# The low half of split weight chunks: negated high half plus an accumulating DMA in place of a VectorE subtraction

## The chip, the cores and the metric

The kernel runs on one core of one Trainium2 chip. The metric is the device time of one execution in microseconds (us); the engines' work is read from a hardware profile of one execution. Engines are named as in the profile: PE is TensorE (PEld its weight loads), DVE VectorE, ACT ScalarE, POOL GpSimd, SP SyncE.

## The reference, cut to what matters

One decoder block on 16 meta tokens and 512 tokens of width 1024. Every large step is a float32 matrix product with a weight matrix:

```python
hn = rmsnorm(h, norm1_g); p = hn @ w_in          # q, k, v, glr, r, u, ga, gb
o = rmsnorm(gla_chunked(q, k, v, log_a)); y_a = (o * silu(r)) @ w_a
y_b = (multiscale_pool(u) @ w_pool_grp * pool_scale) @ w_b
h = h + (sigmoid(ga) * y_a + sigmoid(gb) * y_b) @ w_o
up = causal_dwconv(rmsnorm(h, norm2_g) @ w_up); a, b = split(up)
h = h + (silu(a) * b) @ w_down
out = rmsnorm(h, final_norm_g)
```

## The kernel before, in words

Activations lie transposed, features on the 128 partitions and 528 positions along the row. The weights are cut on the host into 142 chunks `wts[j]` of 128 x 1024 float32 (512 KB): 8 blocks of 128 x 128 that make one block of 128 output features. The order of the chunks, `ORDER`, is k 0-3, q 4-7, v 8-15, r 16-23, u 24-31, ga 32-39, a 40-47, gb 48-55, grp 56-57, b 58-65, o 66-73, up 74-117, down 118-141. In the down stage three chunks make one output block, and the third of the three has only 6 blocks (`nk = 6`, 384 KB).

PE multiplies rounded numbers (`F32R`), so each operand is split into a rounded high part and the rest: `hi = round(w)`, `lo = w - hi`. `products` issues for each block hi x activation-hi, hi x activation-lo and lo x activation-hi, twice each for the two halves of the positions: 48 matmuls for a chunk, the low half needed first by the fifth of them.

The preparation of chunk j is a chain. SP loads `wts[j]` into a raw tile (`wraw`, three buffers); ACT copies it, rounded, into `whi`; DVE subtracts into `wlo` (`whi` and `wlo` have three buffers each). `chunk(j)` prepares chunks up to j + 2 (`PREP_AHEAD`) and loads up to j + 5. So the buffers of chunk j + 2 come free when PE is through with chunk j - 1, that is, as it begins chunk j, and the chain has two chunks' worth of PE time to end. Instructions on one engine run in the order the scheduler of the tile framework gave them, and each waits for its operands by semaphores.

POOL has little to do before the change: constants at the start, the running sums of the pooling branch (line 500, tiles `pt`, 10 additions from the tiles `u` over some 46 us in the u and ga stages), and sums of squares for the last two norms (lines 574 and 627).

Of the kernel before, what the change touches and what calls it, by code (L numbers as in the profile page):

```python
# [13 lines left out]
ALU = mybir.AluOpType  # L14
# [7 lines left out]
KT = 8  # L22
# [23 lines left out]
ORDER = {}  # L46
# [10 lines left out]
def f32(ap):  # L57
    return ap.bitcast(F32)
# [3 lines left out]
def hybrid_block(ctx: ExitStack, tc: tile.TileContext, xt, g1d, wts, wglr, wgk, vecs, out):  # L62
    nc = tc.nc
    act, dve, pool, pe, sp = nc.scalar, nc.vector, nc.gpsimd, nc.tensor, nc.sync
# [19 lines left out]
    def load_chunk(j, cuts=None):  # L84
        if j >= NCHUNK or (j in raws and cuts is None):
            return
        nk = 6 if j >= ORDER["down"] and (j - ORDER["down"]) % 3 == 2 else KT
        if j not in raws:
            raws[j] = (wrawp.tile([P, KT, P], F32, tag="wraw", name=f"wraw{j}"), nk)
        for a, b in cuts or ((0, nk),):  # L90
            sp.dma_start(raws[j][0][:, a:b], wts[j, :, a:b])

    def prep_chunk(j, cuts=None):
        if j >= NCHUNK or (j in preps and cuts is None):
            return
        load_chunk(j)
        t, nk = raws[j]
        if cuts is None or cuts[0] == 0:
            preps[j] = tuple(whlp.tile([P, KT, P], F32R, tag=f"w{n}", name=f"w{n}{j}") for n in ("hi", "lo"))
        hi, lo = preps[j]  # L100
        a, b = cuts or (0, nk)
        act.activation(hi[:, a:b], t[:, a:b], AF.Copy)  # L102
        dve.tensor_tensor(lo[:, a:b], t[:, a:b], f32(hi[:, a:b]), ALU.subtract)  # L103

    def chunk(j, ahead=PREP_AHEAD):
        for i in range(j, j + ahead + 1):
            prep_chunk(i)
        for i in range(j, j + RAW_AHEAD + PREP_AHEAD + 1):
            load_chunk(i)
        return preps[j]  # L110
# [71 lines left out]
    for k in range(KT):  # L182
        for a, b in FULL if k == 0 else ((0, L),):
            act.activation(xh[:, k, a:b], x0[:, k, a:b], AF.Copy, scale=g1[:, k : k + 1])
            dve.scalar_tensor_tensor(xl[:, k, a:b], x0[:, k, a:b], g1[:, k : k + 1], f32(xh[:, k, a:b]), ALU.mult, ALU.subtract)
        for cut in {0: ((0, 2),), 1: ((2, 5),), 3: ((5, 8),)}.get(k, ()):
            prep_chunk(0, cut)
            prep_chunk(1, cut)
        if k >= 2:
            act.activation(sq1[:, k - 2], x0[:, k - 2], AF.Square)  # L190
# [76 lines left out]
    for k in range(KT):  # L267
        for m in range(2):
            hi, lo = preps[m]
# [215 lines left out]
    for g in range(4):  # L485
# [7 lines left out]
        for i in range(g + 1):  # L493
            d = 1 << i
            nxt = pts[g % 2][:, 2 * (2 * (g // 2) + i % 2) :][:, 0:2]
            a = starts[i]
            if a < d:
                pool.tensor_copy(nxt[:, :, a:d], cur[:, :, a:d])
                a = d
# [32 lines left out]
    for m in range(8):  # L532
        hi, lo = chunk(ORDER["grp"] + m // 4)
# [16 lines left out]
    for m in range(8):  # L550
        acc = project(f"pb{m}", ORDER["b"] + m, pbh, pbl, TAIL)
        t = gb[:, m, T0:]
# [9 lines left out]
    for m in range(8):  # L562
        acc = project(f"po2{m}", ORDER["o"] + m, mh, ml, TAIL)
        t = h2[:, m, T0:]
# [66 lines left out]
    for a, b in ((0, 256), (256, 512)):  # L631
# [8 lines left out]
        t = h3[:, 7, a:b]  # L640
# [81 lines left out]
```

## Time and profile before

| | |
|---|---|
| time, median of 3 runs | 862.53 us (862.34 to 862.57) |
| span of the profiled execution | 860.6 us, so 1.9 us of the median lie outside the span |
| PE busy | 847.6 us (98%) |
| PEld busy | 824.5 us (96%) |
| DVE busy | 485.0 us (56%), of it 175.9 us for the 146 subtractions of line 103 |
| ACT busy | 345.1 us (40%), of it 149.2 us for the 146 rounding copies of line 102 |
| POOL busy | 62.3 us (7%) |
| SP's queue of DMAs | 30.4% of the 16 DMA engines' time, 78.84 MB |

The device time of the profiled execution itself isn't given beside its span; its span stands for it, and the 1.9 us are added to it. In a row of a timeline the columns are start, duration, engine, line, operation and tiles. In a row of groups they are count, total time, mean of one, and idle time ahead of it. The row `DMA` of the page gives the busy share of the DMA engines in 40 slices, in tenths.

### The profile page before, as it was taken

How to read it: one execution, taken by the hardware profiler on the slowest of the kernel's cores; microseconds unless marked ns; L12 is line 12 of the kernel's file. 1: busy time of each engine (PE TensorE's matmuls, PEld its weight loads, DVE VectorE, ACT ScalarE, POOL GpSimd, SP SyncE). 2: the span in 40 equal slices, each digit the busy share in tenths (PEclk: the TensorE clock that was granted, in tenths of full speed). 3: DMA queues.
4: the chain of work that ended last, by engine and by line, in shares of the span. 5: the costliest groups of instructions: out<-in, count | busy, mean ns of one | idle time of the engine just before them, and what ended most of it. 6: DMA issues, size and time to landing. Idle time of an engine off the chain costs nothing.

```text
span 860.6 us, 15278 instructions
## 1 busy us (share of the span) xinstructions
PE 847.6 (98%) x6627; PEld 824.5 (96%) x6627; DVE 485.0 (56%) x716; ACT 345.1 (40%) x479; POOL 62.3 (7%) x48
## 2 busy tenths in 40 slices
PE   8999999999999999999999999999999999999995
PEld 7999999999999999999999999999999999888884
DVE  6676445389647433355554677667776777332224
ACT  6378243256335212353234544444444444232231
POOL 4000000001740000000012100000000000001011
PEclk9999999999999999999999999999999999999998
DMA  7423311122332333225332333233323332332312
GB/s 241 123 74 99 87 61 50 50 75 74 99 98 75 98 98 99 84 89 196 98 88 85 99 98 85 89 98 99 90 83 98 98 95 79 95 101 85 97 39 98
DMA packets 25939, 81.13 MB, mean 94 GB/s; under 512 B 2864, under 2 KB 5680, under 8 KB 25872
## 3 DMA queue, kind: packets, MB, share of 16 engines
q1 hardware_dynamic: 24384, 78.84, 30.4%
q10 hardware_dynamic: 1488, 1.32, 0.5%
q8 instruction: 52, 0.85, 0.4%
q14 instruction: 15, 0.12, 0.0%
HBM read 78.05 MB, written 2.10 MB: 93 GB/s over the span
## 4 chain that ended last, share of the span: by engine, by line
PE 96%; DVE 1%; ACT 1%; DMA 1%; issue 0%; SPq 0%; DVEq 0%
PE pup L119 29%; PE pv L119 5%; PE pu L119 5%; PE pr L119 5%; PE pga L119 5%; PE po L119 5%; PE pb L119 5%; PE pgb L119 5%; PE pa L119 5%; PE pd L615 5%; PE pd L614 5%; PE pd L616 5%; PE pq L119 3%; PE pk L119 1%; PE pgrp L119 1%; PE po L415 1%
## 5 line engine op out<-in xcount | busy, mean ns | idle before, releaser
L102 ACT ACTIVATE whi<-wraw 128x1024 fp32r<-128x1024 f32 (+2 forms) x146 | 149.2, 1024 | 330.2 <-PE pd L615 71.0
L103 DVE TENSOR_TENSOR wlo<-wraw,whi 128x1024 fp32r<-128x1024 f32 (+2 forms) x146 | 175.9, 1206 | 78.8 <-ACT whi L102 68.8
L119 PE MATMUL pup<-h2l,whi 128*128 128x258 f32 x704 | 141.6, 282 | 0.0
L119 PE MATMUL pup<-h2h,whi 128*128 128x258 f32 x704 | 140.9, 282 | 0.0
L119 PE MATMUL pup<-h2h,wlo 128*128 128x258 f32 x704 | 140.8, 281 | 0.0
L119 PEld LDWEIGHTS pup<-h2h,wlo 128*128 128x128 f32 x704 | 108.8, 188 | 0.0
L119 PEld LDWEIGHTS pup<-h2h,whi 128*128 128x128 f32 x704 | 107.9, 188 | 0.0
L119 PEld LDWEIGHTS pup<-h2l,whi 128*128 128x128 f32 x704 | 107.8, 188 | 0.0
L614 PE MATMUL pd<-gh,whi 128*128 128x512 f32 (+1 forms) x198 | 72.7, 367 | 0.0
L615 PE MATMUL pd<-gl,whi 128*128 128x512 f32 (+1 forms) x198 | 72.4, 365 | 0.0
L616 PE MATMUL pd<-gh,wlo 128*128 128x512 f32 (+1 forms) x198 | 72.3, 365 | 0.0
L591 DVE TENSOR_TENSOR up<-pup,rstd 128x258 f32<-128x258 f32 x88 | 33.5, 421 | 45.9 <-PE pup L119 44.5
L614 PEld LDWEIGHTS pd<-gh,whi 128*128 128x128 f32 x198 | 37.3, 189 | 6.1
L616 PEld LDWEIGHTS pd<-gh,wlo 128*128 128x128 f32 x198 | 37.3, 189 | 6.0
L615 PEld LDWEIGHTS pd<-gl,whi 128*128 128x128 f32 x198 | 37.3, 189 | 6.0
L594 ACT ACTIVATE cv<-up,vec 128x512 f32<-128x512 f32 x44 | 35.9, 816 | 3.8 <-DVE up L591 3.2
L218 ACT ACTIVATE gh<-cv 128x512 fp32r<-128x512 f32 x22 | 13.9, 633 | 55.1 <-DVE cv L600 55.1
L596 DVE SCALAR_TENSOR_TENSOR cv<-up,vec,cv 128x512 f32<-128x512 f32 x44 | 33.1, 752 | 1.5
L595 DVE SCALAR_TENSOR_TENSOR cv<-up,vec,cv 128x512 f32<-128x512 f32 x44 | 32.9, 747 | 1.3 <-ACT cv L594 1.3
L627 POOL TENSOR_TENSOR sq<-sq,n_sq 128x512 f32<-128x512 f32 x6 | 7.8, 1296 | 348.0 <-ACT n_sq L626 348.0
L598 ACT ACTIVATE cv<-cv 128x512 f32<-128x512 f32 x22 | 13.9, 633 | 41.1 <-DVE cv L596 41.1
L574 POOL TENSOR_TENSOR n_sq<-n_sq,n_sq 128x514 f32<-128x514 f32 x7 | 12.4, 1778 | 220.5 <-ACT n_sq L570 220.5
(241 smaller groups left out, 1804.5 us busy)
## 6 DMA issues: line engine op xcount, KB each, us to landing
wraw<-in_wts_dram SPq DMA_DIRECT2D x132, 512.0 KB, 3.6
wraw<-in_wts_dram SPq DMA_DIRECT2D x10, 384.0 KB, 3.1
h<-in_xt_dram SPq DMA_DIRECT2D x1, 2056.0 KB, 8.8
x<-in_xt_dram SPq DMA_DIRECT2D x7, 264.0 KB, 5.9
out_dram<-h ACTq DMA_DIRECT2D x2, 384.0 KB, 2.8
out_dram<-h ACTq DMA_DIRECT2D x2, 256.0 KB, 2.3
out_dram<-h SPq DMA_DIRECT2D x2, 256.0 KB, 2.5
x<-in_xt_dram SPq DMA_DIRECT2D x2, 132.0 KB, 2.4
```

The costliest lines, as they stand in the source:

```text
L102: act.activation(hi[:, a:b], t[:, a:b], AF.Copy)
L103: dve.tensor_tensor(lo[:, a:b], t[:, a:b], f32(hi[:, a:b]), ALU.subtract)
L119: pe.matmul(acc[:, s, : b - a], w, x[:, a:b], start=(i == 0 and w is wh and x is xh), stop=(i == n - 1 and last),)
L218: act.activation(hi, src, AF.Copy)
L591: dve.tensor_tensor(z[:, c], src, rstd2[:, c], ALU.mult)
L594: act.activation(cv, z[:, META:], AF.Identity, scale=v1("cw2", m), bias=v1("cb", m))
L595: dve.scalar_tensor_tensor(cv, z[:, META - 1 : L - 1], v1("cw1", m), cv, ALU.mult, ALU.add)
L596: dve.scalar_tensor_tensor(cv, z[:, META - 2 : L - 2], v1("cw0", m), cv, ALU.mult, ALU.add)
L598: last = act.activation(cv, cv, AF.Silu)
L614: pe.matmul(acc, hi[:, k], gh[part][:, k, a:b], start=first, stop=False)
L615: pe.matmul(acc, hi[:, k], gl[part][:, k, a:b], start=False, stop=False)
L616: pe.matmul(acc, lo[:, k], gh[part][:, k, a:b], start=False, stop=last)
```

## The change

For chunks 4 to 141, other than the eight with `nk = 6`, DVE no longer subtracts: 130 chunks. In its place the low tile is first set to minus the high tile, by DVE for even j and by POOL for odd j; then POOL issues a DMA that reads the raw chunk from HBM a second time and adds it to what stands in `wlo`. Chunks 0 to 3 and the eight shorter ones keep the subtraction. The raw load by SP and the rounding copy by ACT stay for all chunks.

```diff
         act.activation(hi[:, a:b], t[:, a:b], AF.Copy)
-        dve.tensor_tensor(lo[:, a:b], t[:, a:b], f32(hi[:, a:b]), ALU.subtract)
+        if j < ORDER["q"] or nk < KT:
+            dve.tensor_tensor(lo[:, a:b], t[:, a:b], f32(hi[:, a:b]), ALU.subtract)
+            return
+        if j % 2:
+            pool.tensor_scalar(lo, hi, -1.0, 1.0, ALU.mult, ALU.mult)
+        else:
+            dve.tensor_scalar(lo, f32(hi), -1.0, None, ALU.mult)
+        pool.dma_start(lo, wts[j], accum_op=ALU.add)
```

The new code is seven lines longer, so line 103 of before is line 104 after, and line 500 is 507. PE's and SP's instructions stand in the same order after as before. POOL's don't: it gets 65 negations (line 107) and 130 DMA issues (line 110) among its other work. The number behind a tile's name counts the program's tiles.

First POOL in the u and ga stages. Before, only the additions of the pooling branch stand there:

```order
L500 TENSOR_TENSOR pt_2581<-u 128x2x516
L500 TENSOR_TENSOR pt_2581<-pt_2581 128x2x514
L500 TENSOR_TENSOR pt_2580<-u 128x2x520
L500 TENSOR_TENSOR pt_2580<-pt_2580 128x2x518
L500 TENSOR_TENSOR pt_2580<-pt_2580 128x2x514
L498 COPY pt_2581<-u 128x2
L500 TENSOR_TENSOR pt_2581<-u 128x2x527
L500 TENSOR_TENSOR pt_2581<-pt_2581 128x2x526
L500 TENSOR_TENSOR pt_2581<-pt_2581 128x2x522
L500 TENSOR_TENSOR pt_2581<-pt_2581 128x2x514
L507 TENSOR_SCALAR pt_2581<-pt_2581 128x2
```

After, the weight chunks stand among them; wlo_2367 belongs to chunk 30 and wlo_2431 to chunk 31:

```order
L507 TENSOR_TENSOR pt_2611<-u 128x2x516
L110 DMA wlo_2367<-in_wts_dram 128x1024
L507 TENSOR_TENSOR pt_2611<-pt_2611 128x2x514
L107 TENSOR_SCALAR wlo_2431<-whi_2430 128x1024
L110 DMA wlo_2431<-in_wts_dram 128x1024
```

and a little later wlo_2627 to chunk 34 and wlo_2685 to chunk 35:

```order
L505 COPY pt_2611<-u 128x2
L507 TENSOR_TENSOR pt_2611<-u 128x2x527
L110 DMA wlo_2627<-in_wts_dram 128x1024
L507 TENSOR_TENSOR pt_2611<-pt_2611 128x2x526
L507 TENSOR_TENSOR pt_2611<-pt_2611 128x2x522
L507 TENSOR_TENSOR pt_2611<-pt_2611 128x2x514
L514 TENSOR_SCALAR pt_2611<-pt_2611 128x2
L107 TENSOR_SCALAR wlo_2685<-whi_2684 128x1024
L110 DMA wlo_2685<-in_wts_dram 128x1024
```

So the DMA of chunk 30 stands behind one long addition, and the negation and DMA of chunk 35 behind three.

At the end of the program POOL has, after the change, the negation of chunk 139 (wlo_8643) and the DMAs of chunks 139 and 140 (wlo_8648) ahead of its last sums:

```order
L107 TENSOR_SCALAR wlo_8643<-whi_8642 128x1024
L110 DMA wlo_8643<-in_wts_dram 128x1024
L110 DMA wlo_8648<-in_wts_dram 128x1024
L634 TENSOR_TENSOR sq_8084<-sq_8084,n_sq_8719 128x512
L657 TENSOR_TENSOR h_8083<-h_8083,rstd_0_8798 128x2x256
```

On DVE in the up stage a pair of chunks has two subtractions before (wlo_6494 and wlo_6559), each behind the eviction of an accumulator (`up<-pup`):

```order
L591 TENSOR_TENSOR up_0_6485<-pup_0_6436,rstd_5130 128x258
L591 TENSOR_TENSOR up_0_6485<-pup_0_6436,rstd_5130 128x256
L103 TENSOR_TENSOR wlo_6494<-wraw_6306,whi_6493 128x1024
L595 SCALAR_TENSOR_TENSOR cv_0_6488<-up_0_6485,vec,cv_0_6488 128x512
L596 SCALAR_TENSOR_TENSOR cv_0_6488<-up_0_6485,vec,cv_0_6488 128x512
L591 TENSOR_TENSOR up_1_6548<-pup_1_6499,rstd_5130 128x258
L591 TENSOR_TENSOR up_1_6548<-pup_1_6499,rstd_5130 128x256
L103 TENSOR_TENSOR wlo_6559<-wraw_6369,whi_6558 128x1024
```

After, such a pair has one negation on DVE:

```order
L598 TENSOR_TENSOR up_0_7488<-pup_0_7439,rstd_5202 128x258
L598 TENSOR_TENSOR up_0_7488<-pup_0_7439,rstd_5202 128x256
L602 SCALAR_TENSOR_TENSOR cv_0_7491<-up_0_7488,vec,cv_0_7491 128x512
L603 SCALAR_TENSOR_TENSOR cv_0_7491<-up_0_7488,vec,cv_0_7491 128x512
L598 TENSOR_TENSOR up_1_7552<-pup_1_7503,rstd_5202 128x258
L598 TENSOR_TENSOR up_1_7552<-pup_1_7503,rstd_5202 128x256
L109 TENSOR_SCALAR wlo_7563<-whi_7562 128x1024
```

The other chunk of the pair left DVE's order and stands in POOL's.

## The prediction

> **What bounds the kernel now.** The page first. Its head gives each engine's busy time, and its slices where:
>
> ```profile
> span 860.6 us, 15278 instructions
> PE 847.6 (98%) x6627; PEld 824.5 (96%) x6627; DVE 485.0 (56%) x716; ACT 345.1 (40%) x479; POOL 62.3 (7%) x48
> PE   8999999999999999999999999999999999999995
> DMA  7423311122332333225332333233323332332312
> ```
>
> PE is the bound: idle for 860.6 - 847.6 = 13.0 us, nearly all in the first and last slices. DVE, which the change relieves, is busy for half the time. The windows say how full PE is in the long stages, and the waits of PE, in the row that concerns this change, what the subtractions cost it:
>
> ```profile
> 60.00:120.00 60.00, 60.00 (x499) 60.00 (x498) 32.95 (x61) 30.18 (x71) 0.00 (x0) 1.00 0.30 88
> ...
> 522.00:600.00 78.00, 78.00 (x657) 78.00 (x656) 57.16 (x84) 34.32 (x41) 0.00 (x0) 1.00 0.31 90
> ```
>
> ```profile
> PE pk L119 <- DVE wlo L103: 0.4, 1, 0.4
> ```
>
> Columns: window, length, then busy time and count of PE, PEld, DVE, ACT, POOL, granted clock (1.00 is full), DMA share, GB/s. PE has no gap in either. It waited for a low half once, 0.4 us, on a k chunk, which the change leaves alone. PE's instructions and their order don't change. So there is next to nothing to win; the question is whether the new chain is hidden.
>
> How much time the chain has is read from the timeline of one plain chunk, in the a stage (rows of ACT, DVE and PEld):
>
> ```profile
> 281.23 1.06 ACT L102 ACTIVATE whi<-wraw 128x1024 fp32r<-128x1024 f32 x1 [1.91 <-PE pga L119]
> 281.57 0.31 PEld L119 LDWEIGHTS pa<-zh,wlo 128*128 128x128 f32 x2
> 282.32 1.23 DVE L103 TENSOR_TENSOR wlo<-wraw,whi 128x1024 fp32r<-128x1024 f32 x1 [0.15 <-ACT whi L102]
> 286.95 1.06 ACT L102 ACTIVATE whi<-wraw 128x1024 fp32r<-128x1024 f32 x1 [4.02 <-PE pa L119]
> ...
> 293.01 0.31 PEld L119 LDWEIGHTS pa<-zh,wlo 128*128 128x128 f32 x2
> ```
>
> ACT starts on a chunk as PE lets go of the old one: 281.23, and the next at 286.95, so a chunk takes 5.72 us of PE. The low half whose preparation starts here is the one first loaded at 293.01, two chunks after 281.57. DVE is done at 283.55: 9.46 us to spare.
>
> **The change, part by part.**
>
> *The subtraction goes*, the negation comes. Prices, from groups of DVE and of POOL:
>
> ```profile
> L103 DVE TENSOR_TENSOR wlo<-wraw,whi 128x1024 fp32r<-128x1024 f32 x132 | 165.3, 1253 | 73.6 <-ACT whi L102 63.6
> L646 DVE TENSOR_SCALAR h<-h,vec 128x256 f32<-128x256 f32 x2 | 0.7, 352 | 1.0 <-ACT sq L642 1.0
> L319 DVE TENSOR_SCALAR mid_p<-bn 128x16 f32<-128x16 f32 x1 | 0.2, 172 | 0.0
> L258 POOL MEMSET early_r<- 128x1024 int32 x1 | 1.0, 957 | 0.0
> L500 POOL TENSOR_TENSOR pt<-pt 128x1028 f32<-128x1028 f32 x3 | 8.8, 2931 | 0.2
> L500 POOL TENSOR_TENSOR pt<-pt 128x1036 f32<-128x1036 f32 x1 | 1.9, 1916 | 0.1
> ```
>
> DVE loses 130 x 1.25 = 163 us. A one-input TENSOR_SCALAR goes from 172 ns at 16 columns to 352 at 256, 0.75 ns a column, so 0.9 us at 1024 (bounds 0.35 and 1.25); 65 of them are 60 us. DVE ends near 380 us busy, and this buys nothing, since DVE is waited for by no one that matters. POOL's negation reads one tile: between the memset of that size (1.0) and a two-input addition of that size, 1.9 where it ran free and 2.9 where it ran beside DVE's work. I take 1.2, near the memset as it too has one stream fewer, and keep 2.9. That is 78 us of POOL, 190 at worst, spread over the span.
>
> *The raw tile* is released by ACT instead of DVE, so SP's loads start about 1.2 us sooner. SP waited long there, but the loads were far ahead, and its gain is nothing:
>
> ```profile
> SPq L91 <- DVE wlo L103: 729.5, 134, 12.5
> ```
>
> *The accumulating DMA* has no row before. The nearest are plain loads (size, count, median us from issue to landing):
>
> ```profile
> wraw<-in_wts_dram SPq DMA_DIRECT2D x132, 512.0 KB, 3.6
> ...
> h<-in_xt_dram SPq DMA_DIRECT2D x1, 2056.0 KB, 8.8
> ```
>
> From these, (8.8 - 3.6) / 1544 KB gives 1.7 us of moving for 512 KB and 1.9 us fixed. The window 522:600 agrees: 0.31 of 5.72 us is 1.77 us of all DMA engines for a load. An add reads its target as well as its source. Bounds: 3.6 us if the second read hides, 8.8 if an add costs as much as moving four times the bytes. I take twice the bytes moved, 1.9 + 3.4 = 5.3 us to land, issuing by POOL included, for that is what must be read at least; it is nearer the lower row. The DMA engines are then busy for 1.77 + 3.54 = 5.3 of each 5.72 us, 93%: full, but not over.
>
> The Trainium skill, "Collectives: The Full Stack", section "The bandwidth ceiling: the fold count and why AG ≠ RS ≠ AR", says that an add inside the DMA path costs its second source read and no more; it measured 62.28 GB/s for the copying and 32.35 for the adding collective, a ratio of 1.93. No run here shows it yet; by it the landing would be an estimated 1.9 + 1.93 x 1.7 = 5.2 us, and the sum 0.3 us less. Against the change speaks "DMA: Bandwidth & Descriptors", section "Specifications": the first byte of a DMA issued from GpSimd comes at about 1 us, from SP at about 0.6. By that the landing would be an estimated 5.7, and the sum 1.2 us more.
>
> Even chunk, on the clock of the timeline above: rounding ends at 282.29, negation 283.2, landing 288.5, needed 293.01: 4.5 us over. Odd chunk: negation by 283.5 (285.2 at worst), landing 288.8 (290.5): 2.5 us over at worst; SP's load of 1.7 us at the same time still fits. POOL has time for it: in two chunks, 11.4 us, it has one negation and two issues to do, and each issue waits only for a negation that is done by then.
>
> *Behind POOL's additions* the cover is thinner. The timeline of POOL, of DVE's eviction that the first addition waits for, and PEld's needs:
>
> ```profile
> 213.18 0.75 DVE L233 TENSOR_TENSOR u<-pu,rstd 128x260 f32<-128x260 f32 x2
> 214.08 6.38 POOL L500 TENSOR_TENSOR pt<-u 128x1032 f32<-128x1032 f32 x1 [10.06 <-DVE u L233]
> 220.54 2.76 POOL L500 TENSOR_TENSOR pt<-pt 128x1028 f32<-128x1028 f32 x1
> ...
> 236.48 1.95 POOL L500 TENSOR_TENSOR pt<-u 128x1054 f32<-128x1054 f32 x1 [0.17 <-DVE u L233]
> 238.51 8.15 POOL L500 TENSOR_TENSOR pt<-pt 128x1052 f32<-128x1052 f32 x3
> ```
>
> ```profile
> 224.07 0.31 PEld L119 LDWEIGHTS pu<-xh,wlo 128*128 128x128 f32 x2
> ...
> 252.97 0.31 PEld L119 LDWEIGHTS pga<-xh,wlo 128*128 128x128 f32 x2
> ```
>
> Chunk 30's DMA stands behind the addition that ran from 214.08 to 220.46. One subtraction less on DVE ahead of the eviction brings that end to 219.2; landing 224.5, needed 224.07: late by 0.5 us (0 if the addition takes 1.9 us, 1.7 if it isn't earlier). Chunk 31: the next addition ends at 222.0, negation 223.2, landing 228.5, needed two chunks after chunk 29's need, near 229.9: in time. Chunk 35 has three additions ahead, to 246.7, the small scaling, the negation to 248.1, landing 253.4, needed 252.97: late by 0.4 (0 to 2.1). A late chunk moves the later needs back with it, so I add only these two.
>
> *At the end* the chunks are shorter for PE and nothing follows that could make up. ACT's and PEld's rows:
>
> ```profile
> 823.10 1.06 ACT L102 ACTIVATE whi<-wraw 128x1024 fp32r<-128x1024 f32 x1 [3.10 <-PE pd L615]
> 828.54 1.06 ACT L102 ACTIVATE whi<-wraw 128x1024 fp32r<-128x1024 f32 x1 [4.38 <-PE pd L615]
> ```
>
> ```profile
> 832.77 0.19 PEld L616 LDWEIGHTS pd<-gh,wlo 128*128 128x128 f32 x1
> ...
> 835.65 0.19 PEld L616 LDWEIGHTS pd<-gh,wlo 128*128 128x128 f32 x1
> ```
>
> Chunk 139, odd: 824.16, negation to 825.4 (827.1), landing 830.7 (832.4), needed 832.77: in time. Chunk 140, even: 829.60, negation 830.5, landing 835.8, needed 835.65: late by 0.2 (0 at a landing of 3.6, 3.7 at 8.8).
>
> **The sum**, against the profiled span: 860.6 + 0.5 + 0.4 + 0.2 = 861.7 us, and 1.9 outside the span make 863.6. Against the median of 862.53 that is +0.13%. About 0.2% (1.7 us) is what a measurement of this kernel can tell from no change, so this counts as none, with its own range 862.4 to 867.
>
> **Rivals.** *The DMA engines become the bound* (slower). This one lies at the place I know least. The load takes 1.77 us of each 5.72, so it decides once an add takes over 3.95 us of all engines, 2.2 plain loads; I count 2.0. About 104 chunks run at 5.7 to 5.9 us: v, the last two of r, and u to up; in the rest of r the recurrence leaves room. At three loads' worth, 1.77 + 5.3 = 7.1 us: 1.36 x 104 = 141 us, and in the down stage three loads and two adds take 15.5 us against 15.0 of PE, 4 more: near 1007. At four, 8.85 us: 325 + 33 us, near 1220. For it speaks that 93% leaves no room for a mistake in the one price without a row; against it, that bytes alone don't reach it.
>
> *The chain becomes too long though the engines keep up* (slower): POOL's 2.9 us negation and a landing of 8.8 that is latency. Then an odd low half lands 1.06 + 2.9 + 8.8 = 12.8 us after release, 1.0 past the 11.8 that the timeline allows (281.23 to 293.01). A late chunk gives the next odd one its room, so every fourth of the 104 stalls: 26 us, near 889. It sets in at 7.8 us to land.
>
> *The add lands like a plain load*, in 3.6 us: every lateness above vanishes, and the time stays at 862.5.
>
> **Chances.** The forecast 0.40 (0.26 of it within 0.2%, 0.14 above); all hidden 0.11; DMA engines bound 0.36; chain too long 0.11; faster 0.02, since no wait of PE goes away and its clock stands at 1.00. Within 0.2%: 0.26 + 0.11 = 0.37. Slower: 0.14 + 0.36 + 0.11 = 0.61. The range runs from 861.8 to 1050, an add worth 3.2 loads; above that I leave 0.14, below it 0.02. The forecast is the likeliest single case, though slower is the likelier sign.
>
> **What the profile after would show.** Right: PE's waits name the low half's DMA two or three times in the u, ga and down stages, under 2 us in all; the landing of the adds stands near 5.3 us; the DMA share in the up stage near 0.9; POOL's negation near 1.2 us. Wrong by the engines: DMA share at 1.0 and a chunk longer than 5.72 us all through the up stage, with PE waiting for the DMA at each. Wrong by the chain: DMA share well below 1 and a wait at every fourth chunk. What would undo the forecast is an add that costs the DMA engines more than 2.2 loads, or an issue that holds POOL for more than some 4 us.

## The result and the profile after

| | before | after |
|---|---|---|
| median of the runs, us | 862.43 | 874.86 |
| ratio | | 1.0146, 95% interval 1.0132 to 1.0160 |
| profiled execution: span, us | 860.6 | 873.6 |

The change makes the kernel 1.5% slower. (One execution of a later run, 1031.3 us at a granted clock of 0.75 where that run's ten others show 0.995 to 0.997, is of a slower state and is left out of the times below.) The page of the changed kernel has these lines where the prediction showed those of before (the queue lines are packets, MB, share of 16 engines; the last two are size, count, median us from issue to landing):

```profile
span 873.6 us, 15546 instructions
PE 852.6 (98%) x6627; PEld 828.2 (95%) x6627; DVE 384.7 (44%) x651; ACT 345.0 (39%) x479; POOL 238.3 (27%) x243
PEclk9999999999899999999999999999999999999998
q0 software_dynamic: 18720, 68.17, 48.5%
wraw<-in_wts_dram SPq DMA_DIRECT2D x132, 512.0 KB, 3.9
wlo<-in_wts_dram POOLq DMA_DIRECT2D x130, 512.0 KB, 6.6
```

DVE gave up 100 us of work, and the span grew by 13.0. PE itself became 5 us busier with the same 6627 matmuls, so some of them ran slower, and the clock row has an 8 in its eleventh slice, from 218 us on. The long stage is as the prediction drew it. Columns of the window: length, busy time and count of PE, PEld, DVE, ACT, POOL, granted clock, DMA share, GB/s:

```profile
522.00:600.00 78.00, 78.00 (x657) 78.00 (x656) 46.13 (x77) 34.20 (x41) 18.94 (x21) 1.00 0.88 183
```

PE has no gap there and a full clock, beside DMA engines that are busy for 0.88 of the time. The waits of PE say where the loss is (us in total, times, longest):

```profile
PE pu L126 <- DMA wlo<-in_wts_dram: 4.1, 1, 4.1
PE pga L126 <- DMA wlo<-in_wts_dram: 2.6, 1, 2.6
...
PE pb L126 <- DMA wlo<-in_wts_dram: 0.7, 1, 0.7
```

A fourth, 0.3 us, is in the down stage. They sum to 7.7 us, not 13. PE's order is the same in both kernels, so the start of each matmul can be set against its start before; the lag grows at four places and hardly elsewhere:

| place, us of the span | chunk | stop | slower matmuls behind it | lost |
|---|---|---|---|---|
| 218.4, u stage | 29 | 4.28 | 2.55 | 6.83 |
| 260.0, ga stage | 35 | 2.77 | 1.44 | 4.21 |
| 412.9, b stage | 61 | 0.85 | 0.10 | 0.95 |
| 848.1, down stage | 140 | 0.46 | 0.10 | 0.56 |

12.5 of the 13.0 us. The second column of losses is the clock. Windows right behind the first two stops:

```profile
222.80:228.30 5.50, 5.46 (x25) 5.46 (x26) 2.27 (x5) 1.41 (x2) 1.92 (x2) 0.50 0.60 139
262.80:265.70 2.90, 2.84 (x13) 2.84 (x14) 0.00 (x0) 0.00 (x0) 0.19 (x1) 0.50 1.04 285
```

The granted clock is 0.50, and the first window holds 25 matmuls; the same 5.5 us of the kernel before, at full clock, hold 47.

How the first stop came about is told by the timelines of ACT, POOL, DVE and PEld, in this order:

```profile
209.69 1.05 ACT L102 ACTIVATE whi<-wraw 128x1024 fp32r<-128x1024 f32 x1
```
```profile
210.82 4.71 POOL L107 TENSOR_SCALAR wlo<-whi 128x1024 fp32r<-128x1024 f32 x1 [5.54 <-ACT whi L102]
215.83 0.88 POOL L110 DMA_DIRECT2D wlo<-in_wts_dram  x1 [0.30 <-POOL wlo L107]
```
```profile
209.70 1.29 DVE L486 TENSOR_TENSOR o<-o,r 128x514 f32<-128x514 f32 x2
210.91 1.29 DVE L226 TENSOR_TENSOR zl<-o,zh 128x514 fp32r<-128x514 f32 x2
212.12 0.68 DVE L486 TENSOR_TENSOR o<-o,r 128x514 f32<-128x514 f32 x1
212.72 1.89 DVE L226 TENSOR_TENSOR zl<-o,zh 128x514 fp32r<-128x514 f32 x3
214.53 0.75 DVE L240 TENSOR_TENSOR u<-pu,rstd 128x260 f32<-128x260 f32 x2
```
```profile
222.84 0.50 PEld L126 LDWEIGHTS pu<-xh,wlo 128*128 128x128 f32 x2 [4.33 <-DMA wlo<-in_wts_dram]
```

POOL's negation is on the books from 210.82 to 215.53, while DVE works without a break on operations that read two SBUF tiles; they end at 214.5 (the row after them reads an accumulator, `pu`, and one SBUF tile), and the negation ends 1.0 us later, which is what it takes when alone. So it stood still behind them. ACT's copy was late before that, and for the same reason the other way round: the `zh` copies ahead of it wait for DVE, and DVE was held while an addition of POOL ran (timelines of POOL and DVE):

```profile
203.06 2.22 POOL L507 TENSOR_TENSOR pt<-u 128x1028 f32<-128x1028 f32 x1
203.45 2.39 DVE L213 SCALAR_TENSOR_TENSOR osq<-osq 128x514 f32<-128x514 f32 x1
```

That operation of DVE takes 0.70 us in the run below that has the additions on DVE. Counted from the same eviction on DVE (200.36 here), the copy starts after 9.33 us, in that run after 8.82 and in the kernel before after 8.77. The DMA was issued at 215.83 and landed 6.97 us later; PE had stopped at 218.5. The second stop has another start, POOL's own queue (timeline of POOL):

```profile
247.13 6.74 POOL L507 TENSOR_TENSOR pt<-pt 128x1052 f32<-128x1052 f32 x3
253.96 0.23 POOL L514 TENSOR_SCALAR pt<-pt 128x2 f32<-128x2 f32 x1
254.17 1.05 POOL L107 TENSOR_SCALAR wlo<-whi 128x1024 fp32r<-128x1024 f32 x1
255.51 1.79 POOL L110 DMA_DIRECT2D wlo<-in_wts_dram  x2 [0.30 <-POOL wlo L107]
```

Two DMAs go out together behind the three additions, and the first lands at 262.81.

### The profile page after: what moved, and what is told of

Its sections match the earlier page's. It is cut to its first block, busy times and chain, and to the rows that moved or that the text cites. A ratio compares the mean times of both kernels' runs of the same rounds, so it can differ in the third digit from the quotient of the medians.

```text
span 873.6 us, 15546 instructions
## 1 busy us (share of the span) xinstructions
PE 852.6 (98%) x6627; PEld 828.2 (95%) x6627; DVE 384.7 (44%) x651; ACT 345.0 (39%) x479; POOL 238.3 (27%) x243
## 3 DMA queue, kind: packets, MB, share of 16 engines
q0 software_dynamic: 18720, 68.17, 48.5%
## 4 chain that ended last, share of the span: by engine, by line
PE 89%; DMA 4%; DVE 2%; POOL 1%; ACT 1%; issue 1%; SPq 0%; DVEq 0%; ACTq 0%
PE pup L126 29%; PE pv L126 5%; PE pr L126 5%; PE po L126 5%; PE pgb L126 5%; PE pa L126 5%; PE pd L623 4%; PE pd L621 4%; PE pd L622 4%; PE pb L126 4%; PE pu L126 4%; PE pga L126 3%; DMA wlo<-in_wts_dram 3%; PE pq L126 3%; PE pk L126 1%; PE pgrp L126 1%
## 5 line engine op out<-in xcount | busy, mean ns | idle before, releaser
L110 POOL DMA_DIRECT2D wlo<-in_wts_dram x130 | 114.0, 878 | 336.2 <-issue 210.0
L107 POOL TENSOR_SCALAR wlo<-whi 128x1024 fp32r<-128x1024 f32 x65 | 75.3, 1159 | 244.3 <-ACT whi L102 244.3
L109 DVE TENSOR_SCALAR wlo<-whi 128x1024 fp32r<-128x1024 f32 x65 | 48.8, 750 | 59.0 <-ACT whi L102 54.6
L602 DVE SCALAR_TENSOR_TENSOR cv<-up,vec,cv 128x512 f32<-128x512 f32 x44 | 34.9, 793 | 22.8 <-ACT cv L601 20.7
L603 DVE SCALAR_TENSOR_TENSOR cv<-up,vec,cv 128x512 f32<-128x512 f32 x44 | 33.1, 752 | 1.5
L126 PE MATMUL pu<-xh,wlo 128*128 128x258 f32 (+3 forms) x128 | 27.1, 294 | 4.1 <-DMA wlo<-in_wts_dram 4.1
## 6 DMA issues: line engine op xcount, KB each, us to landing
h<-in_xt_dram SPq DMA_DIRECT2D x1, 2056.0 KB, 15.7
```

The source lines that it names most:

```text
L107: pool.tensor_scalar(lo, hi, -1.0, 1.0, ALU.mult, ALU.mult)
L109: dve.tensor_scalar(lo, f32(hi), -1.0, None, ALU.mult)
L110: pool.dma_start(lo, wts[j], accum_op=ALU.add)
L126: pe.matmul(acc[:, s, : b - a], w, x[:, a:b], start=(i == 0 and w is wh and x is xh), stop=(i == n - 1 and last),)
L602: dve.scalar_tensor_tensor(cv, z[:, META - 1 : L - 1], v1("cw1", m), cv, ALU.mult, ALU.add)
L603: dve.scalar_tensor_tensor(cv, z[:, META - 2 : L - 2], v1("cw0", m), cv, ALU.mult, ALU.add)
```

## The experiments

Theory A: the loss is made at a few chunks, 29 and 35 above all, where the new steps meet the pooling additions on POOL's queue and DVE's two-input work; each late chunk stops PE once, and the clock then costs more. Everywhere else the chain is hidden. Theory B: the DMA engines, near full, land the adds too late wherever something small disturbs them, so POOL's order matters little and a cost stays with every chunk. Diffs are against the changed kernel unless said otherwise; each run stands beside runs of the kernel before on the same chip (medians 862.26 to 862.72).

**The old subtraction for chunks 29 to 35.**

```diff
-        if j < ORDER["q"] or nk < KT:
+        if j < ORDER["q"] or nk < KT or 29 <= j <= 35:
```

> Chunks 29 to 35 keep the subtraction of before; the other 123 changed chunks stay as changed. Theory A (the loss is made at two places, chunk 29 and chunk 35, where the odd negation and the DMA issue meet the pooling additions on POOL and two-input work on DVE, and PE's clock halves after each gap): both gaps and their slow stretches go, 7.1 + 4.1 us, so 863 to 864.5 us, and PE waits for the low half's DMA for under 1.5 us in all. Theory B (the DMA engines, busy for near 0.9 of the time, land the adds too late, and where POOL's work stands matters little): other chunks near them become late instead, 870 us or more.

864.99 us, ratio 1.0032 (1.0020 to 1.0043). Seven chunks of 130 hold 9.9 of the 12.4 us. No wait for a low half is left in u and ga; what is left for the most part is the b stage:

```profile
PE pb L126 <- DMA wlo<-in_wts_dram: 1.3, 1, 1.3
```

That is theory A's case, half a microsecond above its upper end.

**POOL negates the even chunks, DVE the odd.**

```diff
-        if j % 2:
+        if j % 2 == 0:
```

> Even chunks are negated by POOL and odd ones by DVE, so chunks 29 and 35 get DVE's negation; the count of each is the same. Theory A, with the blocked POOL negation (4.71 us) as the larger part of the loss at chunk 29: the negation there takes under 1.5 us, the gap falls from 4.1 to about 1.4 us; chunk 35 keeps three additions ahead of its DMA and saves only the 1.05 us negation, gap 1.3 to 1.6. In all 865 to 868 us. If instead the late rounding copy (ACT) or the landing makes the gap at chunk 29: above 871. Theory B: 873 to 876, no change.

871.48 us, ratio 1.0107 (1.0091 to 1.0124): better than the changed kernel, but not as far as theory A had it; above 871 was expected for a late copy or a long landing. The waits that stay:

```profile
PE pu L126 <- DMA wlo<-in_wts_dram: 3.4, 1, 3.4
PE pga L126 <- DMA wlo<-in_wts_dram: 1.7, 1, 1.7
```

Chunk 29's negation is DVE's now and takes 0.69 us. But it began only at 212.82, behind the gating's operations in DVE's queue; the DMA went out at 214.04, 1.8 us sooner than in the changed kernel, and took 8.62 us to land, 1.65 more than there; why the landing grew wasn't tested. So the blocked negation is one cause of lateness at this place and not the whole.

**All negations on DVE.**

```diff
-        if j % 2:
+        if False:
```

> All 130 negations on DVE, none on POOL, which only issues the DMAs. Theory A: as with the swapped turns at chunks 29 and 35, and no even chunk can be blocked either: 864.5 to 867.5 us. DVE's busy time grows by 65 x 0.7 = 45 us and costs nothing. Theory B: 873 to 876.

867.86 us, ratio 1.0067 (1.0050 to 1.0084), 0.4 us above the range of theory A. Two stops of 1.5 us in the u stage, three below 1 us elsewhere, and no slow matmuls behind any: what is lost is the stops alone, 5 us. POOL is a bad place for the negation, but its queue still holds every DMA issue.

**The pooling additions on DVE instead of POOL.**

```diff
-            pool.tensor_tensor(nxt[:, :, a:], cur[:, :, a:], cur[:, :, a - d : L - d], ALU.add)
+            dve.tensor_tensor(nxt[:, :, a:], cur[:, :, a:], cur[:, :, a - d : L - d], ALU.add)
```

(and the small copy ahead of them.)

> The ten additions of the pooling branch move from POOL to DVE, so nothing long stands ahead of the DMA issues in the u and ga stages; POOL keeps the odd negations. Theory A says chunk 35's gap goes with its slow stretch (4.1 us). Chunk 29: if the negation there is blocked by DVE's two-input work, it stays blocked, and the time is 868 to 872; if POOL's own additions ahead of it and beside DVE are what delays it, that goes too, and the time is 863 to 865. Theory B: 873 to 876.

868.78 us, ratio 1.0082 (1.0062 to 1.0103). The stop in ga is gone; the one in u is not, as POOL's timeline shows:

```profile
209.87 3.52 POOL L107 TENSOR_SCALAR wlo<-whi 128x1024 fp32r<-128x1024 f32 x1 [6.97 <-ACT whi L102]
```

No addition is near it, and it takes 3.5 us: DVE's two-input operations end at 212.4 in this run, and the negation ends at 213.4, again 1.0 us later. So chunk 35 is late through POOL's own additions, chunk 29 through DVE's work.

**A plain DMA in place of the accumulating one** (the low half becomes the whole raw chunk; the subtraction is left out).

```diff
-        pool.dma_start(lo, wts[j], accum_op=ALU.add)
+        pool.dma_start(lo, wts[j])
```

> Every chunk's low-half DMA overwrites instead of adding (the subtraction is left out: the low half becomes the whole raw chunk); negations, queue and issue times stay. It prices the addition alone. If adding costs a second read of 512 KB, the queue's share falls from 48.5% to about half, 25%, and the landing from 6.6 us to 3.9 to 5. Theory A (lateness at two places): the landing is 1.6 to 2.7 us shorter, so chunk 29 still stops PE, by 4.3 less that, 1.6 to 2.7 us, chunk 35 by 0 to 1.2, nothing in the branch products; 865 to 868 us. Theory B (DMA engines near full): the time returns to before, 862 to 864 us, with no stall left.

864.41 us in one run, between the ranges of the two theories. The page has the price of adding:

```profile
q0 software_dynamic: 18720, 68.17, 27.3%
wraw<-in_wts_dram SPq DMA_DIRECT2D x132, 512.0 KB, 3.5
wlo<-in_wts_dram POOLq DMA_DIRECT2D x130, 512.0 KB, 4.7
```

27.3% of a span of 862.7 us over 130 chunks is 1.81 us of the engines, against 48.5% of 873.6, 3.26 us, with the addition: 1.8 times as much, and 1.9 us more to land. One stop is left, chunk 29, 2.17 us, at a full clock, which is what theory A gave for it. So the wait on ACT and POOL makes chunk 29 late even when nothing is added; the addition makes it 2.1 us worse, and makes chunks 35, 61 and 140 late.

**One more accumulating DMA for each up chunk, into a spare tile** (the lines that make and clear the tile are left out here).

```diff
+        if ORDER["up"] <= j < ORDER["down"]:
+            pool.dma_start(spare, wts[j], accum_op=ALU.add)
```

> In the up-projection each of the 44 chunks gets a second accumulating DMA into a spare tile that nothing reads. By the measured shares an addition holds the 16 engines for 3.26 us and a load for about 1.7, so a chunk would need 1.7 + 2 x 3.3 = 8.2 us of engines against 5.72 us of PE. If the engines' share is real work, PE is slowed to that: 44 x 2.5 = 109 us longer, 970 to 990 us, DMA share 1.0 through the stage. If the share counts waiting that overlaps (engines shown busy but not full), the stage hides part: below 920 us, and at 875 all of it.

979.29 us, the number that was forecast, and for another reason. The spare tile waits for nothing, so the extra DMAs were put far ahead in POOL's order: they went out from 13.5 to 289.8 us, before the up stage, each waiting for the one before it to land. The group of POOL (busy, mean ns, idle before):

```profile
L114 POOL DMA_DIRECT2D spare<-in_wts_dram x44 | 38.2, 868 | 203.8 <-DMA spare<-in_wts_dram 194.2
```

For 194 us POOL stood at one of them, with the low halves' DMAs queued behind. It shows what a waiting DMA issue does to its queue, and nothing of the engines' limit.

**The same, tied to its place:** half of a chunk's high part is negated once more on DVE into one of two spare half tiles, and an accumulating DMA of half a chunk goes onto it (the line that makes their pool is left out here).

```diff
+        if ORDER["up"] <= j < ORDER["down"]:
+            spare = sparep.tile([P, KT // 2, P], F32R, tag="spare", name=f"spare{j}")
+            dve.tensor_scalar(spare, f32(hi[:, : KT // 2]), -1.0, None, ALU.mult)
+            pool.dma_start(spare, wts[j, :, : KT // 2], accum_op=ALU.add)
```

> Again the limit of the DMA engines, with the extra work now tied to its place: in the up-projection each of the 44 chunks negates half of its high part once more on VectorE into one of two spare half tiles, and an accumulating DMA of half a chunk is added to it; nothing reads them. In this stage a chunk holds the engines for 0.88 x 5.72 = 5.0 us (measured); half an addition more is 1.6 us, so 6.6 us against 5.72 us of PE. If the shown share is work that can't be packed closer, PE waits 0.9 us per chunk: about 40 us longer than the changed kernel, 905 to 920 us, DMA share 1.0. If a good part of the share is waiting that overlaps, the stage hides it: 875 to 885 us.

875.19 us in one run, 0.3 us above the changed kernel: half an addition more per chunk cost nothing. The window of the up stage, and the landings:

```profile
522.00:600.00 78.00, 78.00 (x656) 77.89 (x655) 52.59 (x91) 34.22 (x41) 32.24 (x34) 1.00 1.03 229
```
```profile
wlo<-in_wts_dram POOLq DMA_DIRECT2D x130, 512.0 KB, 6.9
spare<-in_wts_dram POOLq DMA_DIRECT2D x44, 256.0 KB, 7.4
```

The share rises from 0.88 to 1.03 and the traffic from 183 to 229 GB/s, PE still without a gap. A share of 0.88 was thus not 88% of what the engines can do; the times counted for packets overlap, or the share couldn't pass 1. Theory B falls as a limit of the long stages. A crowd of DMAs at one place can still make a landing long, as at chunk 61 (below).

**Stops without the change:** the kernel before, with DVE's subtraction repeated for some chunks. First try:

```diff
-        dve.tensor_tensor(lo[:, a:b], t[:, a:b], f32(hi[:, a:b]), ALU.subtract)
+        for _ in range({42: 10, 47: 11, 52: 12, 63: 14}.get(j, 1)):
+            dve.tensor_tensor(lo[:, a:b], t[:, a:b], f32(hi[:, a:b]), ALU.subtract)
```

> The kernel before, with VectorE's subtraction of four chunks repeated (chunk 42 ten times, 47 eleven times, 52 twelve times, 63 fourteen times), so that PE is stopped by about 1.6, 2.9, 4.1 and 6.5 us with no accumulating DMA and no POOL work in the chain. If a stop alone halves the clock afterwards: matmuls at half speed for some microseconds behind the stops of 4.1 and 6.5, none behind 1.6, and the one of 2.9 tells on which side it falls; 2.5 to 3 us are lost behind each, so 862.4 + 15 + 5 to 8 = 882 to 886 us. If the half clock in the changed kernel had to do with its own traffic, no slow matmuls follow, 877 to 878 us.

868.09 us: the slack swallowed more than reckoned, no stop was longer than 1.6 us, and no slow matmuls followed. It left the question open, so the repeats were made longer:

```diff
-        dve.tensor_tensor(lo[:, a:b], t[:, a:b], f32(hi[:, a:b]), ALU.subtract)
+        for _ in range({42: 15, 90: 17, 105: 20}.get(j, 1)):
+            dve.tensor_tensor(lo[:, a:b], t[:, a:b], f32(hi[:, a:b]), ALU.subtract)
```

> The kernel before, with VectorE's subtraction repeated 15 times for chunk 42, 17 for chunk 90, 20 for chunk 105: stops of PE of about 3, 5 and 9 us without any accumulating DMA or POOL work. If a stop of more than some 2.5 us is enough to halve the clock: 1.4 to 2.8 us are lost behind each of the three in matmuls that take twice as long, and 862.5 + 17 + 6 = 885 us. If the slow matmuls need the changed kernel's traffic, none follow: about 880 us.

885.18 us, the number that was forecast for a halving by the stop alone, but partly by luck, as the stops fell otherwise: chunk 42's repeats made none, 90's two, of 3.4 and 2.9 us, 105's one of 5.2, together 11.5 and not 17; waits of up to 1.1 us for ACT's copy came beside them. The three long stops were each followed by slow matmuls, 2.9, 1.8 and 2.4 us lost; the short waits were not. A window behind the longest:

```profile
674.00:679.00 5.00, 4.85 (x22) 4.85 (x23) 5.00 (x8) 0.82 (x1) 0.00 (x0) 0.50 0.33 105
```

The clock is 0.50 with POOL idle and a DMA share of 0.33. The stop alone does it.

**The old subtraction for the four chunks that showed a stop.**

```diff
-        if j < ORDER["q"] or nk < KT:
+        if j < ORDER["q"] or nk < KT or j in (29, 35, 61, 140):
```

> The changed kernel with the old subtraction kept for chunks 29, 35, 61 and 140 (four of 130). Theory A: all four places that showed a stop are taken away and the 126 others stay hidden: 862.6 to 863.6 us, within 0.2% of before. A rival to the reading of the run that kept it for 29 to 35: the neighbours 30, 31 and 33, which go through POOL's queue again here, then stop PE in their turn, 1 to 4 us: 864 to 868 us.

867.10 us, ratio 1.0045 (1.0031 to 1.0059): the rival reading. Chunk 30 stops PE in its turn (waits of PE, then POOL's timeline):

```profile
PE pu L126 <- DMA wlo<-in_wts_dram: 2.7, 1, 2.7
```
```profile
215.31 6.45 POOL L507 TENSOR_TENSOR pt<-u 128x1032 f32<-128x1032 f32 x1 [10.07 <-DVE u L240]
221.71 0.87 POOL L110 DMA_DIRECT2D wlo<-in_wts_dram  x1
```

A stop of 2.90 us and 1.6 us of slow matmuls. In the changed kernel chunk 29's stop had covered it. There the addition took 2.21 us and chunk 30's DMA went out at 218.31 and landed at 225.25; without the stop PE would have needed it at 224.25, with the stop it needed it at 231.07.

**The negation reads the raw chunk**, not the high part that ACT writes.

```diff
-            pool.tensor_scalar(lo, hi, -1.0, 1.0, ALU.mult, ALU.mult)
+            pool.tensor_scalar(lo, t, -1.0, 1.0, ALU.mult, ALU.mult)
-            dve.tensor_scalar(lo, f32(hi), -1.0, None, ALU.mult)
+            dve.tensor_scalar(lo, t, -1.0, None, ALU.mult)
```

> The changed kernel with the negation reading the raw chunk instead of the high part (written as fp32r, so it is rounded as the high part is): it no longer waits for ACT's rounding copy, and in POOL's order chunk 29's negation now stands before the pooling additions' first. Theory A says that ACT's late copy begins the loss at chunk 29: its stop of 4.3 us and the slow matmuls behind it (6.8 us together) go, chunk 35, which is late behind POOL's additions whatever the negation reads, keeps 2 to 4 us: 866 to 869 us. If ACT's copy was not what delayed it, but the buffers coming free or the landing, the time stays at 873 to 876.

874.97 us, ratio 1.0148 (1.0134 to 1.0161): as slow as the changed kernel, and the expectation missed. Chunk 29 is in time now; its DMA went out at 209.44. But chunk 30's was behind the addition again:

```profile
217.26 5.85 POOL L507 TENSOR_TENSOR pt<-u 128x1032 f32<-128x1032 f32 x1 [5.00 <-DVE u L240]
223.05 0.88 POOL L110 DMA_DIRECT2D wlo<-in_wts_dram  x1
```

PE stopped at 225.1 for 3.4 us, and at chunk 35 for 3.6, whose DMA, out at 253.47 and thus 2.0 us sooner than in the changed kernel, took 9.28 us to land. Over the whole run the landings grew too, which wasn't explained:

```profile
wlo<-in_wts_dram POOLq DMA_DIRECT2D x130, 512.0 KB, 7.7
```

ACT's late copy chose which chunk was late; POOL's queue made one late in any case.

**The old subtraction for chunks 29 to 35, 61 and 140.**

```diff
-        if j < ORDER["q"] or nk < KT:
+        if j < ORDER["q"] or nk < KT or 29 <= j <= 35 or j in (61, 140):
```

> The changed kernel with the old subtraction kept for chunks 29 to 35, 61 and 140, nine of 130. Theory A: with the two places, their neighbours and the two small stops taken away nothing is left: 862.4 to 863.2 us, the same as before, though 121 chunks still go through negation and accumulating DMA. Theory B (a cost on every chunk, from the DMA engines or otherwise): at least 2 us stay, 865 us or more.

863.19 us (median of ten), ratio 1.0013 (1.0003 to 1.0022): at the upper end that A gave. PE waits for no low half's DMA any more. 121 chunks still go through negation and accumulating DMA, and by the interval they cost 0.3 to 1.9 us together. Theory A holds as to where the loss is made; how long each landing takes stays a part of it. No version beat the kernel before: PE is the bound, and no run gave it less to do.

## Why the prediction was right and where it was wrong

Right: there was nothing to win, and the steady state hides the chain. DVE ended at 384.7 us busy (380 forecast), a negation cost 0.75 us on DVE and 1.16 on POOL (0.9 and 1.2), the DMA share was 0.88 (0.93), the engines' time per addition 3.26 us (3.54). The sign that got the larger chance came, and the time lies in the stated range of 861.8 to 1050. Both were in good part luck: the range was that wide, and 0.47 of the 0.61 for slower stood, because of a bound by the DMA engines and a chain too long at every fourth chunk, and neither came; the way that came, a few late chunks, had 0.14 for a time clear of no change. The forecast case is right in kind, a few late chunks in the u, ga and down stages, and wrong in size: 863.6 against 874.86 us, outside its own range of 862.4 to 867. PE's waits for the low half came at four places and not two or three, the b stage among them, and summed to 7.7 us and not under 2.

The steps that failed:

*Which chunk is late in the u stage.* The prediction checked odd chunks on a plain one of the a stage and took chunk 29 for in time. Its own prices, set into the rows of before, would have said the same; ACT's copy of that chunk, and PE's need of it:

```profile
208.95 1.04 ACT L102 ACTIVATE whi<-wraw 128x1024 fp32r<-128x1024 f32 x1
...
218.26 0.31 PEld L119 LDWEIGHTS pu<-xh,wlo 128*128 128x128 f32 x2
```

209.99 + 1.2 + 5.3 = 216.5, so 1.8 us to spare. Measured, ACT's copy came 0.74 later, the negation with the steps around it took 5.1 us and the landing 6.97: 222.80, a stop of 4.28 us. That the copy could come later, through DVE, was not reckoned with.

*POOL's negation "at worst 2.9".* That bound came from a two-input addition beside DVE. Alone the negation is about 1.05 us, but here it gave way to DVE for as long as DVE's two-input operations followed each other without a break: 4.71 us. The rows of before already held this. The addition that the prediction shows at 214.08 took 6.38 us, and it ended at 220.46, 1.9 us (its price alone) behind the end of such a train on DVE:

```profile
216.80 1.89 DVE L219 TENSOR_TENSOR zl<-o,zh 128x514 fp32r<-128x514 f32 x3
218.61 0.76 DVE L233 TENSOR_TENSOR u<-pu,rstd 128x262 f32<-128x262 f32 x2
```

The bound should have been a train's length and not 2.9. The Trainium skill, "SBUF — State Buffer", section "Who interferes with whom", states the exclusion: a DVE instruction with two SBUF inputs and a GpSimd instruction that reads SBUF contend for a shared port, which is locked for one of them. The rows of 210 to 215 us agree, and those of 203 us show the other order.

*The landing of 5.3 us.* The median is 6.6; at the places that matter 6.97, 7.30 and, for chunk 61, 9.82. The fixed part was taken from SP's loads, but a plain DMA from POOL's queue lands in 4.7 us against 3.5 for SP's in the same run, and the addition takes 1.9 more. Why chunk 61's was so long wasn't tested. The likely cause is a load that the prediction left out: SP's load of h (2056 KB) went out at 402.63, 1.4 us ahead of chunk 61's DMA, and landed in 15.7 us, against 8.8 before, and meanwhile the traffic was high:

```profile
404.00:414.00 10.00, 9.31 (x79) 9.11 (x77) 4.21 (x9) 2.76 (x3) 2.00 (x3) 1.00 1.01 286
```

*The terms.* Chunk 35: 0.4 forecast, a stop of 2.77 measured; the additions ahead of it ended at 253.9, and the landing gave 2 us more. Chunk 30: 0.5 forecast, 0 in the changed kernel, but 2.90 once chunk 29 no longer covered it, since the addition ended at 221.7 and not at 219.2. Chunk 140: 0.2, measured 0.46. Chunk 61: none, 0.85.

*What a stop costs.* The sum took each lateness once. Behind the two long stops the halved clock added 2.55 and 1.44 us, 4.0 of the 13.0.

*The rivals.* The DMA engines did not become the bound, and the point at which they would, 2.2 plain loads, was reckoned from a share that is no measure of fullness: 1.03 was shown with nothing lost. The price of an addition, 1.8 copies, lies near the doubling that was taken. The chain that is too long at every fourth chunk didn't come either: its condition was a negation of 2.9 us and a landing of 7.8, and the negation took 1.16 in the mean and the landing 6.6 in the median. And that the addition would land like a plain load and cost nothing had the wrong time: with plain DMAs chunk 29 still stopped PE, for 864.4 and not 862.5.

## What to carry to other kernels

When a hidden preparation gets longer, check each chunk at which the engine or queue of a new step has other work, on that chunk's own rows, not on a plain chunk; and add up the whole in-order queue, since a DMA issue waits like any instruction. If PE, as the bound engine, stops for 2.8 us or more, add another 1.4 to 2.8 us for its clock. Undoing the change for the few suspected chunks shows at once whether the cost lies there or in every chunk, but undo the neighbours too: the first stop hides the second.

## What was not expected of the hardware

Between which stops the clock halves came out sharply. Over the changed kernel, its variants and the repeated subtractions, every stop of 2.75 us and more was followed by matmuls at half speed, 1.4 us lost at least; none of 2.17 us and less was. Between these two no stop was seen. The stretches of half clock in the changed kernel, cut out as windows (the clock stands after the busy times):

```profile
221.53:228.34 6.81, 5.50 (x25) 5.50 (x26) 3.54 (x7) 2.19 (x3) 1.92 (x2) 0.50 0.69 151
262.49:265.88 3.39, 3.02 (x14) 3.02 (x15) 0.00 (x0) 0.00 (x0) 0.50 (x1) 0.50 1.05 280
```

They last 6.83 and 3.41 us and begin 40.96 apart, and in the other traces too such stretches last 3.41 us or a multiple and begin multiples of 3.41 apart. So the clock changes on a fixed beat and not a fixed time after the stop begins: it fell 2.8 us after PE's last matmul at the first stop, 2.2 us after it at the second, and, with the additions on DVE, only 1.1 us after PE had begun again (220.87, 221.92). What a stop costs hangs on where it falls in that beat: in the run with the extra DMAs far ahead, stops of 4.0 and 4.1 us were followed by losses of 2.8 and 1.6 us. The Trainium skill, "TensorE: Matmul & The Clock Gate", section "Part 1: The HAM clock gate (the "warmup" mystery)", has the half rate set in after an idle window of about 3.4 us, and full rate come back after as long a busy one. The traces differ on the first: stops of 2.75 us were enough, and the clock fell after 2.2 us of idleness. On the second they are near in one case: full clock came back 3.0 us after PE had begun again at the second stop, but 5.5 us after it at the first.

An accumulating DMA of 512 KB into SBUF took 1.8 times the engines' time of the same DMA without the addition, and 6.6 us instead of 4.7 to land. The DMA share of a window can pass 1: 1.03 over 78 us at 229 GB/s, with no wait of PE in that window.
